# A two-layer decoder trunk on one Trainium2 core: where the sink's exponential lands, and what the turned squares and GpSimd's masks wait for

## The chip, the cores and the metric

The kernel runs on one core of one Trainium2 chip. The core has five engines, each with its own queue of instructions that it works off in order: TensorE (PE in the profile; its loading of weights is listed apart as PEld), VectorE (DVE), ScalarE (ACT), GpSimd (POOL) and SyncE (SP), which here only issues DMA transfers. Data lies in SBUF; matrix products arrive in PSUM, in banks of 512 float32 columns on 128 partitions. The metric is the device time of one execution in microseconds. The kernel before took 1000.27 us, the median of three runs (999.51 to 1000.80).

## What is computed

A trunk of two layers on 512 tokens of width 1024, in float32. Layer A has latent attention with 8 heads, layer B sliding-window attention with 16 query heads on 4 key/value heads, with a learned sink per head; each is followed by an MLP of width 4096 with a squared ReLU. Every sublayer ends in a layer norm of `alpha*x + y`. The part that the change touches is layer B's attention:

```python
def _swa(x, w_q, sinks, w_o, k_band, v_band, rel_bias):
    ...
    s = jnp.where(mask[None, :, None, None], s + bias, -jnp.inf)
    sink = sinks.astype(jnp.float32).reshape(SWA_KV_HEADS, G)[..., None]
    m = jnp.maximum(s.max(-1), sink)
    p = jnp.exp(s - m[..., None])
    denom = p.sum(-1) + jnp.exp(sink - m)
    p = (p / denom[..., None]).astype(x.dtype)
    o = jnp.einsum('bnkgqj,bnjkd->bnqkgd', p, v_band).reshape(B, S, SWA_Q_HEADS * SWA_HEAD_DIM)
    return o @ w_o
```

Queries go in 4 blocks of 128; each block sees the keys of its own block and the one before, 128 back at most.

## The kernel before

**Split factors.** Every float32 operand of a product is held as a high and a low part, and a product is made as two or three matrix products of parts. The helper `split` (L77 and L81) makes the parts: ScalarE copies the source into the high part, and VectorE, or GpSimd where the caller says so, subtracts it from the source to get the low part. All products go through `group` (L105). Weights come in 512 KB pieces by DMA and are split the same way, into tiles `wh` and `wl`; for layer B's query weights from the third piece on and for some pieces of the output projection, GpSimd makes the low part.

**Order.** Instructions are put in order on each engine when the kernel is built, by a planner that simulates the engines with a cost model: of what is ready it takes what comes first in the program, and `high_priority` moves an instruction ahead. `pe(...)` keeps instructions of one engine in program order; all of TensorE's work here is pinned so. `behind((a,))` puts the instructions in its block behind instruction `a` on the same engine. Once built, an engine's order is fixed: an instruction that waits holds all that stand behind it on its engine.

**Layer B's attention.** `run_steps` goes over 16 heads, one step for each. Step u calls `scores(u + 2)`, then pieces of other work from a list (the query projection of two heads at a time, parts of the output projection from step 11 on), then `turn(u)`, and in every second step `mix` for the pair of heads before.

- `scores(h)` makes the four blocks of scores in two PSUM banks `bs[0]` and `bs[1]`, each block with the keys of the block before (128 columns) and its own (128 columns). As exactly one of the two is in reach for each pair of positions, `copy_predicated` (L1426) lays the reachable part of the older block over the own one, so that a head has squares of 128 x 128: one for each query block. VectorE adds the bias and takes the maximum (L1430); `nb` (L1434) is the negated, scaled maximum with the sink. Block 0 has no older block, so the first 128 columns of `bs[0]` are free; the maxima `mx` lie in columns 0 to 3.
- `weigh(h)` takes four exponentials on ScalarE (L1445), each with its sum into `sm`, then the sink's exponential into `ri` (L1449). VectorE adds the two (L1450) and inverts the sum (L1451). GpSimd scales the squares `p` (L1452). For heads 12 to 14, `scores` only appends the head to `waiting`, and `weigh` is called at the end of the next `turn`.
- `turn(h)` transposes the four squares on TensorE (L1468) into a bank of `tbank`, splits it into the tile `pt` (`split`: ScalarE, then VectorE), and GpSimd multiplies three of the squares by the triangle `tri` into `pm` (L1472). For heads 0 to 9 ScalarE's copy in this split is put behind the latest exponential in the program, that of head h + 2 (`state["exp"]`).
- `mix(h)` multiplies the values by `pt` and `pm` of two heads; its first half goes to a bank of `tbank`, its second to one of `bank`. ScalarE copies the upper partitions (L1502, `low`), VectorE adds (L1504, `o`), and `split` with GpSimd makes `oh` and `ol`, the factors of the output projection.

`tbank` has two buffers and `bank` six. [...]

Of the kernel before, what the change touches and what calls it, by code (L numbers as in the profile page):

```python
# [10 lines left out]
AF = mybir.ActivationFunctionType  # L11
# [4 lines left out]
P = 128  # L16
D = 1024
S = 512
NT = S // P
# [6 lines left out]
SQH, SKVH, SHD = 16, 4, 64  # L26
# [22 lines left out]
def build(tc, nc, io, out):  # L49
    with ExitStack() as top:  # L50
# [11 lines left out]
        def nm(s):  # L62
            n_names[0] += 1
            return f"{s}_{n_names[0]}"

        def bank(cols=512, tag="mm", bufs=6):
            return ps.tile([P, cols], F32, tag=tag, bufs=bufs, name=nm(tag), padded_shape=[P, 512])

        def tbank():
            return bank(512, "tr", 2)  # L70

        def f32(ap):
            return ap.bitcast(F32)

        def split(dst_h, dst_l, src, engine=None, keep=False):

            high = nc.scalar.activation(dst_h, src, AF.Copy)  # L77
            if keep:
                pe(high)
            with behind(state.pop("open", None)):  # L80
                low = (engine or nc.vector).tensor_sub(dst_l, src, f32(dst_h))  # L81
            if pinned[0] and engine is None:
                pe(low)
            return high, low

        def pe(ins):
            tc.keep_in_program_order(ins)
# [3 lines left out]
        def behind(pair):  # L91

            both = ExitStack()
            for ins in pair or ():
                both.enter_context(tc.issue_after(ins.ins))
            return both
# [6 lines left out]
        def group(dst, pairs, first=True, last=True, **kw):  # L103
            for i, (st, mv) in enumerate(pairs):
                pe(nc.tensor.matmul(  # L105
                    dst, st, mv, start=first and i == 0, stop=last and i == len(pairs) - 1, **kw
                ))
# [214 lines left out]
        state = {"next": 0, "at": 0, "hold": 0}  # L322
# [32 lines left out]
        class Feat:  # L355
# [11 lines left out]
            def turn(self, t):  # L367
                turn_tokens(t, self)
# [59 lines left out]
        sink = cp.tile([P, SQH], F32, name="sink")  # L428
# [167 lines left out]
        def run_steps(units, ahead, scores, turn, mix, fill, per, lag, rest):  # L596

            total = sum(f[0] for f in fill)  # L600
            n, spent, at = len(units), 0.0, 0
            for u in range(-ahead, n):
                if u + ahead < n:
                    scores(*units[u + ahead])
                target = total * (u + ahead + 1) / (n + ahead)
                while at < len(fill) and (spent < target or fill[at][1] <= u) and fill[at][2] <= u:
                    fill[at][3]()
                    spent += fill[at][0]
                    at += 1
                if u < 0:  # L610
                    continue
                turn(*units[u])
                if u >= lag and (u - lag) % per == per - 1:
                    mix(units[u - lag][0])
            for f in fill[at:]:
                f[3]()
            for f in rest:
                f()
            for u in range(n, n + lag):
                if (u - lag) % per == per - 1:  # L620
                    mix(units[u - lag][0])
# [338 lines left out]
        with tc.tile_pool(name="mla", bufs=1) as mp:  # L960
# [123 lines left out]
            for t in range(NT):  # L1084
# [12 lines left out]
                if t == 2:  # L1097
                    with tc.high_priority():
                        pt = tbank()
# [186 lines left out]
            for t in range(2):  # L1286
                for kp in range(3):
                    fill.append((1.3, 99, max(8 * kp + 10, 29 * t), lambda t=t, kp=kp: proj.part(t, kp)))
                    if t == kp == 0:
# [3 lines left out]
            state["hold"] = hold  # L1293
            head_queries(1)
            run_steps([(h, i) for h in range(H) for i in range(NT)], AHEAD_S, scores, turn, mix, fill, NT, 2,
                      [lambda kp=kp: proj.part(2, kp) for kp in range(2)])

# [18 lines left out]
        with tc.tile_pool(name="swa", bufs=1) as mp:  # L1316
# [56 lines left out]
            bias = [None] * 8  # L1373
# [24 lines left out]
                    nc.scalar.activation(q[own, cols], b[own, :], AF.Copy)  # L1398
                    nc.vector.tensor_sub(q[other, cols], b[own, :], f32(q[own, cols]))  # L1399

            ps_of = [None] * SQH
            pts = [None] * 8

            def scores(h, _):
                j = h // GRP
                q = qs[h]
                nb = sp.tile([P, NT], F32, tag="nb", bufs=3, name=nm("nb"))
                sm = sp.tile([P, NT], F32, tag="sm", bufs=3, name=nm("sm"))
                ri = sp.tile([P, NT], F32, tag="ri", bufs=3, name=nm("ri"))
                bs = []  # L1410
                for n2 in range(2):
                    b = bank().rearrange("p (a b) -> p a b", a=2)
                    bs.append(b)
                    for a in range(2):
                        n = 2 * n2 + a
                        lo_c = P if n == 0 else 0
                        kc = slice(0, P) if n == 0 else slice((n - 1) * P, (n + 1) * P)
                        tq = slice(n * P, (n + 1) * P)
                        group(b[:, a, lo_c:], [(q[:, tq], khh[j][:, kc]), (q[:, tq], kll[j][:, kc])])

                mx = bs[0][:, 0, 0:NT]
                for n2 in range(2):
                    at = slice(1 - n2, 2)
                    b = bs[n2][:, at, :]
                    other = upper.bitcast(mybir.dt.int16)[:, None, :].broadcast_to([P, n2 + 1, P])
                    nc.vector.copy_predicated(b[:, :, P:], other, b[:, :, 0:P])  # L1426
                    for a in range(2):
                        n = 2 * n2 + a
                        own = bs[n2][:, a, P:]
                        nc.vector.tensor_tensor_reduce(  # L1430
                            out=own, in0=own, in1=bias[h // 2][:, h % 2, P:] if n == 0 else bias[h // 2][:, h % 2, 0:P],
                            op0=ALU.add, op1=ALU.max, scale=1.0, scalar=NEG, accum_out=mx[:, n : n + 1],
                        )
                nc.vector.tensor_scalar(nb, mx, sink8[:, h : h + 1], -SWA_SCALE, ALU.max, ALU.mult)  # L1434
                if 12 <= h < 15:
                    waiting.append((h, bs, nb, sm, ri))
                else:
                    weigh(h, bs, nb, sm, ri)

            waiting = []  # L1440

            def weigh(h, bs, nb, sm, ri):
                p = mp.tile([P, NT, P], F32, tag="p", bufs=3, name=nm("p"))
                for n in range(NT):
                    state["exp"] = nc.scalar.activation(  # L1445
                        p[:, n, :], bs[n // 2][:, n % 2, P:], AF.Exp, bias=nb[:, n : n + 1],
                        scale=SWA_SCALE, accum_out=sm[:, n : n + 1],
                    )
                nc.scalar.activation(ri, nb, AF.Exp, bias=sink[:, h : h + 1])  # L1449
                nc.vector.tensor_add(sm, sm, ri)  # L1450
                nc.vector.reciprocal(ri, sm)  # L1451
                nc.gpsimd.tensor_mul(p, p, ri.unsqueeze(2).broadcast_to([P, NT, P]))  # L1452
                ps_of[h] = p

            def turn(h, _):
                m, a = h // 2, h % 2
                p = ps_of[h]
                if a == 0:
                    whole = mp.tile([P, 2, NT, 2, P], F32R, tag="pt", bufs=2, name=nm("pt"))
                    if m % 2:  # L1460
                        part = mp.tile([P, 2, NT - 1, 2, P], F32R, tag="pm", bufs=1, name=nm("pm"))
                    else:
                        part = gp.tile([P, 2, NT, 2, P], F32R, tag="gb", bufs=1, name=nm("pm"))[:, :, 1:]
                    pts[m] = whole, part
                whole, part = [z[:, :, :, a, :] for z in pts[m]]
                pt = tbank().rearrange("p (a b) -> p a b", a=NT)
                for n in range(NT):
                    pe(nc.tensor.transpose(pt[:, n, :], p[:, n, :], ident))  # L1468
                with behind((state["exp"],) if h < 10 else None):
                    split(whole[:, 0], whole[:, 1], pt)  # L1470
                own = tri[:, None, None, :].broadcast_to([P, 2, NT - 1, P])
                nc.gpsimd.tensor_mul(part, f32(whole[:, :, 1:]), own)  # L1472
                if waiting:
                    weigh(*waiting.pop())

            def mix(h):
                m, j = h // 2, h // GRP
# [172 lines left out]
```

## Time and profile before

| | us |
|---|---|
| median of three runs (999.51 to 1000.80) | 1000.27 |
| the profiled execution | 999.92 |
| its span, from first to last instruction | 998.1 |

| engine | busy in the span, us | in instructions |
|---|---|---|
| TensorE, products (PE) | 981.4 | 6028 |
| VectorE (DVE) | 780.5 | 1279 |
| ScalarE (ACT) | 545.0 | 842 |
| GpSimd (POOL) | 240.6 | 207 |

Layer B's attention with its first head's scores to its last mix lies between 536 and 636 us of the span. The granted clock of TensorE is 0.999 of full speed over the span.

How to read the rows that follow. A row of a timeline has the start and the duration in us, the engine, the line and the operation, the tile written and the tiles read, their shapes, how many instructions are merged in it, and in brackets the idle time of the engine just before it with what ended that. The name `tr` stands for banks of `tbank`, `mm` for banks of `bank`, also where these hold `mix`'s products. A row of waits says who waited for whom, the sum in us, how often, and the longest. A row of stretches has for each engine the busy time in us and the count of instructions, then the granted clock, the share of DMA and GB/s. A row of groups has the count, the busy time with the mean in ns, and the idle time before. A row of a tile has the shortest, median and longest duration in ns. The chain of waits is what ended last, followed back; "issue" in it is time for which the profile shows no cause.

### The profile page before, as it was taken

The numbers are of one execution on the slowest core, as the hardware profiler recorded it, in microseconds if no ns is written. First come the engines' busy times: TensorE is split into PE (matmuls) and PEld (weight loads), VectorE is DVE, ScalarE is ACT, GpSimd is POOL, SyncE is SP. The second block draws the span as 40 slices with busy tenths as digits, with TensorE's granted clock in tenths as the row PEclk, the third lists the DMA queues.
The fourth block names the chain that finished last, engine by engine and source line by source line (L and its number), as shares of the span: only waits on it lengthen the run. The fifth ranks groups of instructions, "written<-read, shape, count | busy, mean of one in ns | idle before, by whom it ended". The sixth has DMA issues, their size and how long they took to land.

```text
span 998.1 us, 15676 instructions
## 1 busy us (share of the span) xinstructions
PE 981.4 (98%) x6028; PEld 881.4 (88%) x6028; DVE 780.5 (78%) x1279; ACT 545.0 (55%) x842; POOL 240.6 (24%) x207
## 2 busy tenths in 40 slices
PE   9999999999999999999999987999999999999997
PEld 9888888998898999998898876889998999999986
DVE  6589858989679779785686888698885986898756
ACT  5557643567447537646146776436763664664620
POOL 0231101121312212210003887622131122122000
PEclk9999999999999999999999999999999999999999
DMA  7421236399789878954132224237996897898332
GB/s 261 141 91 43 89 123 202 53 214 245 137 206 224 157 169 236 222 91 148 64 106 96 85 70 153 81 89 129 272 190 117 231 217 118 221 263 146 83 127 84
DMA packets 60678, 149.54 MB, mean 150 GB/s; under 512 B 5259, under 2 KB 10300, under 8 KB 60604
## 3 DMA queue, kind: packets, MB, share of 16 engines
q0 software_dynamic: 24320, 58.73, 33.5%
q1 hardware_dynamic: 36140, 89.56, 26.2%
q8 instruction: 47, 0.77, 0.3%
q14 instruction: 27, 0.22, 0.1%
q10 hardware_dynamic: 144, 0.26, 0.1%
HBM read 146.41 MB, written 4.22 MB: 151 GB/s over the span
## 4 chain that ended last, share of the span: by engine, by line
PE 90%; DVE 5%; ACT 3%; issue 1%; POOL 1%; DMA 0%; DVEq 0%; ACTq 0%; POOLq 0%
PE mm L105 83%; PE tr L105 5%; ACT p L1445 1%; DVE sm L1450 1%; DVE o L1504 1%; PE tr L1243 1%; DVE mm L1430 1%; PE tr L742 1%; DVE pt L81 0%; POOL wl L81 0%; DVE mm L1426 0%; ACT wh L77 0%; DMA raw<-in_w_h 0%; PE tr L507 0%; DVE q L1399 0%
## 5 line engine op out<-in xcount | busy, mean ns | idle before, releaser
L105 PE MATMUL mm<-wh,fac 128*128 128x512 f32 (+1 forms) x944 | 292.6, 386 | 0.0
L77 ACT ACTIVATE wh<-wq 128x1024 fp32r<-128x1024 f32 x164 | 173.7, 1060 | 184.6 <-PE mm L105 133.3
L81 DVE TENSOR_TENSOR wl<-wq,wh 128x1024 fp32r<-128x1024 f32 x164 | 199.5, 1220 | 69.6 <-ACT wh L77 68.8
L105 PE MATMUL mm<-xth,wh 128*128 128x256 f32 (+1 forms) x928 | 243.5, 290 | 0.2 <-DVE o L1504 0.2
L105 PE MATMUL mm<-xth,wl 128*128 128x256 f32 (+1 forms) x800 | 233.3, 292 | 0.0
L105 PEld LDWEIGHTS mm<-wh,fac 128*128 128x128 f32 x944 | 176.3, 188 | 35.5 <-DVE fac L81 0.6
L105 PE MATMUL mm<-xtl,wh 128*128 128x256 f32 (+1 forms) x672 | 197.1, 293 | 0.0
L105 PE MATMUL mm<-wl,fac 128*128 128x512 f32 (+1 forms) x472 | 182.3, 386 | 0.0
L105 PEld LDWEIGHTS mm<-xth,wh 128*128 128x128 f32 x928 | 168.6, 192 | 3.4 <-ACT wh L77 0.3
L105 PEld LDWEIGHTS mm<-xth,wl 128*128 128x128 f32 x800 | 153.2, 192 | 2.7
L105 PEld LDWEIGHTS mm<-xtl,wh 128*128 128x128 f32 x672 | 128.7, 191 | 3.0
L77 ACT ACTIVATE wh<-raw 128x1024 fp32r<-128x1024 f32 (+3 forms) x86 | 84.9, 988 | 80.4 <-PE mm L105 54.3
L204 POOL DMA_DIRECT2D wq<-in_up x64 | 77.6, 1238 | 199.5 <-DVE wl L81 192.3
L105 PEld LDWEIGHTS mm<-wl,fac 128*128 128x128 f32 x472 | 88.8, 188 | 16.6
L81 DVE TENSOR_TENSOR wl<-raw,wh 128x1024 fp32r<-128x1024 f32 (+2 forms) x64 | 74.7, 1176 | 31.0 <-ACT wh L77 30.2
L204 POOL DMA_DIRECT2D wq<-in_down x48 | 42.0, 875 | 189.8 <-DVE wl L81 184.0
L81 POOL TENSOR_TENSOR wl<-raw,wh 128x1024 fp32r<-128x1024 f32 (+2 forms) x22 | 47.0, 2138 | 88.0 <-ACT wh L77 65.2
L105 PE MATMUL mm<-wh,oh 128*128 128x512 f32 x128 | 50.8, 397 | 0.0
L105 PE MATMUL mm<-wh,ol 128*128 128x512 f32 x128 | 50.2, 392 | 0.6 <-POOL ol L81 0.6
L443 POOL TENSOR_TENSOR rs<-mv,half 128x1 f32<-128x1 f32 x16 | 10.0, 623 | 166.9 <-DVE mv L488 162.2
L105 PE MATMUL mm<-wl,oh 128*128 128x512 f32 x128 | 50.0, 391 | 0.1
L641 DVE TENSOR_TENSOR x<-mm,x 128x512 f32<-128x512 f32 (+1 forms) x49 | 32.9, 675 | 15.2 <-PE mm L105 15.1
(246 smaller groups left out, 1796.1 us busy)
## 6 DMA issues: line engine op xcount, KB each, us to landing
wq<-in_up POOLq DMA_DIRECT2D x64, 512.0 KB, 7.4
wq<-in_down POOLq DMA_DIRECT2D x48, 512.0 KB, 7.3
wq<-in_up SPq DMA_DIRECT2D x32, 512.0 KB, 6.5
raw<-in_down SPq DMA_DIRECT2D x28, 512.0 KB, 5.7
wq<-in_down SPq DMA_DIRECT2D x24, 512.0 KB, 5.3
raw<-in_up SPq DMA_DIRECT2D x16, 512.0 KB, 4.9
raw<-in_w_o SPq DMA_DIRECT2D x8, 512.0 KB, 3.4
raw<-in_w_sq SPq DMA_DIRECT2D x8, 512.0 KB, 3.2
```

What stands on the lines that cost most here:

```text
L77: high = nc.scalar.activation(dst_h, src, AF.Copy)
L81: low = (engine or nc.vector).tensor_sub(dst_l, src, f32(dst_h))
L105: pe(nc.tensor.matmul(dst, st, mv, start=first and i == 0, stop=last and i == len(pairs) - 1, **kw))
L204: state["added", key, a, more, jp] = nc.gpsimd.dma_start(half(a, jp), chunk(*more, jp), accum_op=ALU.add)
L443: state["rs"] = nc.gpsimd.tensor_tensor(r, v, half, ALU.pow)
L641: nc.vector.tensor_add(xs[t][:, c], b, xs[t][:, c])
L742: pe(nc.tensor.transpose(pt[:, a, :], xs[t][:, k * P : (k + 1) * P], ident))
L1243: pe(nc.tensor.transpose(pt[:, kb * P : (kb + 1) * P], p[:, kb * P : (kb + 1) * P], ident))
L1430: nc.vector.tensor_tensor_reduce(out=own, in0=own, in1=bias[h // 2][:, h % 2, P:] if n == 0 else bias[h // 2][:, h % 2, 0:P], op0=ALU.add, ...
L1445: state["exp"] = nc.scalar.activation(p[:, n, :], bs[n // 2][:, n % 2, P:], AF.Exp, bias=nb[:, n : n + 1], scale=SWA_SCALE, accum_out=sm[: ...
L1450: nc.vector.tensor_add(sm, sm, ri)
L1504: nc.vector.tensor_add(o[to, n2, :].rearrange("p (n q) -> p n q", n=2), parts[lo, :, a, :], low[:, :, a, :],)
```

## The change

Three things are changed, all in layer B's attention. `turn` no longer puts its split behind exponentials, and the deferral of `weigh` for heads 12 to 14 is gone: `scores` always calls `weigh`. The sink's exponential is written to columns 4 to 7 of `bs[0]`, and VectorE's sum reads it there; `ri` then only holds the inverse. GpSimd's scaling is given high priority and kept in `muls`, and the mask of head h is put behind the scaling of head h + 1 on GpSimd's queue. The instructions that are executed are the same in kind and number.

```diff
-            ps_of = [None] * SQH
+            ps_of, muls = [None] * SQH, [None] * SQH
...
                 nc.vector.tensor_scalar(nb, mx, sink8[:, h : h + 1], -SWA_SCALE, ALU.max, ALU.mult)
-                if 12 <= h < 15:
-                    waiting.append((h, bs, nb, sm, ri))
-                else:
-                    weigh(h, bs, nb, sm, ri)
-
-            waiting = []
+                weigh(h, bs, nb, sm, ri)
 
             def weigh(h, bs, nb, sm, ri):
                 p = mp.tile([P, NT, P], F32, tag="p", bufs=3, name=nm("p"))
                 for n in range(NT):
-                    state["exp"] = nc.scalar.activation(
+                    nc.scalar.activation(
                         p[:, n, :], bs[n // 2][:, n % 2, P:], AF.Exp, bias=nb[:, n : n + 1],
                         scale=SWA_SCALE, accum_out=sm[:, n : n + 1],
                     )
-                nc.scalar.activation(ri, nb, AF.Exp, bias=sink[:, h : h + 1])
-                nc.vector.tensor_add(sm, sm, ri)
+                own = bs[0][:, 0, NT : 2 * NT]
+                nc.scalar.activation(own, nb, AF.Exp, bias=sink[:, h : h + 1])
+                nc.vector.tensor_add(sm, own, sm)
                 nc.vector.reciprocal(ri, sm)
-                nc.gpsimd.tensor_mul(p, p, ri.unsqueeze(2).broadcast_to([P, NT, P]))
+                with tc.high_priority():
+                    muls[h] = nc.gpsimd.tensor_mul(p, p, ri.unsqueeze(2).broadcast_to([P, NT, P]))
                 ps_of[h] = p
...
                     pe(nc.tensor.transpose(pt[:, n, :], p[:, n, :], ident))
-                with behind((state["exp"],) if h < 10 else None):
-                    split(whole[:, 0], whole[:, 1], pt)
+                split(whole[:, 0], whole[:, 1], pt)
                 own = tri[:, None, None, :].broadcast_to([P, 2, NT - 1, P])
-                nc.gpsimd.tensor_mul(part, f32(whole[:, :, 1:]), own)
-                if waiting:
-                    weigh(*waiting.pop())
+                with behind((muls[h + 1],) if h + 1 < SQH else None):
+                    nc.gpsimd.tensor_mul(part, f32(whole[:, :, 1:]), own)
```

## The prediction

> **What bounds the kernel now.** I read the engines and the 40 slices of the page first, to find where TensorE (PE) is not busy; then busy time by stretches, the waits of PE, the timeline of one pair of heads, and the chain of waits.
>
> ```profile
> PE 981.4 (98%) x6028; PEld 881.4 (88%) x6028; DVE 780.5 (78%) x1279; ACT 545.0 (55%) x842; POOL 240.6 (24%) x207
> PE   9999999999999999999999987999999999999997
> ```
>
> PE is the bound of the whole, idle for 998.1 - 981.4 = 16.7 us. Apart from the last slice, it drops below 9 tenths only in two slices near 575 to 625 us: layer B's attention, where every edit lies.
>
> ```profile
> core 0: us, PE busy (x) PEld busy (x) DVE busy (x) ACT busy (x) POOL busy (x), PEclk, DMA share, GB/s
> 550.00:570.00 20.00, 19.20 (x118) 16.72 (x117) 16.26 (x59) 12.91 (x41) 18.47 (x11) 1.00 0.32 107
> 570.00:605.00 35.00, 31.25 (x188) 26.89 (x187) 30.78 (x106) 24.92 (x80) 28.33 (x19) 1.00 0.33 112
> 605.00:630.00 25.00, 19.20 (x110) 15.65 (x110) 19.74 (x60) 15.58 (x52) 16.35 (x12) 1.00 0.18 66
> 581.37:592.77 11.40, 10.14 (x62) 8.75 (x61) 9.76 (x35) 8.20 (x26) 9.32 (x7) 1.00 0.20 70
> ```
>
> PE's idle time is 0.80, 3.75 and 5.80 us in the three stretches: 10.35 us, the most that the change can win while PE's work stays. The last row is one pair of heads, from the transposes of head 6 to those of head 8: 10.14 us of PE's work take 11.40, and no engine is full. What PE waited for in these 80 us (us in total, times, longest):
>
> ```profile
> PE tr L105 <- DVE pt L81: 7.4, 5, 2.2
> PE mm L105 <- DVE q L1399: 1.1, 1, 1.1
> PE tr L105 <- DVE nb L1434: 0.8, 1, 0.8
> PE mm L105 <- POOL ol L81: 0.6, 1, 0.6
> PE tr L1468 <- POOL p L1452: 0.3, 1, 0.3
> ```
>
> Four fifths is `mix` (the tile `tr` at L105) waiting for the split of turned squares (`pt`): `mix` takes its first bank from `tbank`, which has two, so it needs the bank of the head turned two uses earlier, free once VectorE (DVE) has made the low part. The pair from the timeline:
>
> ```profile
> 581.37 0.60 PE L1468 MATMUL tr<-ident,p 128*128 128x128 f32 x4
> 584.08 0.35 ACT L1445 ACTIVATE p<-mm,nb 128x128 f32<-128x128 f32 x1
> 585.63 0.59 ACT L77 ACTIVATE pt<-tr 128x512 fp32r<-128x512 f32 x1
> 586.25 0.59 ACT L1398 ACTIVATE q<-mm 64x512 fp32r<-64x512 f32 x1
> 586.54 0.66 DVE L81 TENSOR_TENSOR pt<-tr,pt 128x512 fp32r<-128x512 f32 x1
> 586.77 1.04 POOL L1452 TENSOR_TENSOR p<-p,ri 128x512 f32<-128x512 f32 x1 [0.45 <-DVE ri L1451]
> 587.24 0.69 DVE L1399 TENSOR_TENSOR q<-mm,q 64x512 fp32r<-64x512 f32 x1
> 587.35 0.70 PE L105 MATMUL tr<-pt,vv 128*128 128x512 f32 x2 [1.26 <-DVE pt L81]
> 587.77 1.86 POOL L1472 TENSOR_TENSOR pm<-pt,tri 128x768 fp32r<-128x768 f32 x1
> 588.60 1.04 DVE L1450 TENSOR_TENSOR sm<-sm,ri 128x4 f32<-128x4 f32 x1 [0.67 <-ACT ri L1449]
> 590.10 1.04 POOL L1452 TENSOR_TENSOR p<-p,ri 128x512 f32<-128x512 f32 x1 [0.47 <-DVE ri L1451]
> ```
>
> Head 6 is turned at 581.97, but ScalarE (ACT) splits it at 585.63, behind head 8's exponentials: the written wait. And the sum of four numbers at L1450 takes 1.04 us: it ends at 589.64, when GpSimd's (POOL) mask ends (587.77 + 1.86 = 589.63). The tile's view, with `nb`, an operation as small that reads the bank, and a group row:
>
> ```profile
> L1450 DVE TENSOR_TENSOR sm<-sm,ri x13: 164/1016/1828, 557.8 to 623.0; 128x4 f32<-128x4 f32 x13
> L1434 DVE TENSOR_SCALAR nb<-mm,sink x13: 208/221/224, 555.7 to 621.0; 128x4 f32<-128x4 f32 x13
> L1450 DVE TENSOR_TENSOR sm<-sm,ri 128x4 f32<-128x4 f32 x13 | 12.2, 942 | 4.8 <-ACT ri L1449 4.6
> ```
>
> The sum takes 0.16 us at best and 1.83 at worst. The chain of waits runs through ACT and DVE here, not PE:
>
> ```profile
> 584.08 1.48 ACT p L1445 x8
> 585.56 0.19 ACT ri L1449
> 588.60 1.05 DVE sm L1450
> 595.50 1.48 ACT p L1445 x8
> ```
>
> From one exponential of a pair to the next pair's is 11.42 us, with a stopped sum in it.
>
> **The change part by part.** **The sink's exponential into the bank.** No instruction is added or removed; L1449 writes and L1450 reads four columns of PSUM in place of SBUF. The sum then has one input in SBUF, like `q<-mm,q`: the row at 587.24 takes 0.69 us though the mask starts in its midst. I price the sum at `nb`'s 0.22; ends 0.16 and today's 0.94. For 13 sums that frees 12.2 - 13 x 0.22 = 9.3 us of DVE, of which a pair's chain holds 1.04 - 0.22 = 0.82. ACT's write into a bank has no row; between the sink's exponential as it stands in the chain (0.19) and one of 128 columns (0.35), I take 0.19, as nothing about its length changes; 0.16 more for 13 heads would be 2.1 us of ACT's work, inside its idle time. The 0.06 us by which a bank read exceeds 0.16 (13 x 0.06 = 0.8) lie in DVE's idle time, 11.40 - 9.76 = 1.64 a pair; without that cover 0.8 would be lost.
>
> ```profile
> 589.07 0.22 PE L105 MATMUL mm<-skh,q 128*128 128x128 f32 x1
> 607.01 0.58 ACT L77 ACTIVATE pt<-tr 128x512 fp32r<-128x512 f32 x1
> 609.64 1.86 POOL L1472 TENSOR_TENSOR pm<-pt,tri 128x768 fp32r<-128x768 f32 x1 [2.81 <-DVE pt L81]
> 609.68 1.83 DVE L1450 TENSOR_TENSOR sm<-sm,ri 128x4 f32<-128x4 f32 x1
> 609.71 0.70 PE L105 MATMUL tr<-pt,vv 128*128 128x512 f32 x2 [2.16 <-DVE pt L81]
> 612.44 0.69 DVE L1399 TENSOR_TENSOR q<-mm,q 64x512 fp32r<-64x512 f32 x1
> 613.19 0.39 PE L105 MATMUL mm<-skh,q 128*128 128x256 f32 x1 [1.14 <-DVE q L1399]
> 619.24 0.69 PE L105 MATMUL tr<-pt,vv 128*128 128x512 f32 x2 [1.60 <-DVE pt L81]
> 622.99 1.28 DVE L1450 TENSOR_TENSOR sm<-sm,ri 128x4 f32<-128x4 f32 x1 [1.16 <-ACT ri L1449]
> 628.95 0.50 PE L105 MATMUL mm<-wh,ol 128*128 128x512 f32 x1 [0.63 <-POOL ol L81]
> ```
>
> The bank is held longer: from the last exponential that reads it to the sum. Head 8's exponentials start at 584.08, so its sum can end by 584.08 + 1.48 + 0.19 + 0.22 = 585.97; head 10's scores start at 589.07, so some 3 us remain. [...]
>
> **No wait for the exponentials (heads 0 to 9).** ACT's split, 0.62 us from start to start (585.63 to 586.25), leaves its place between two heads' exponentials. ACT idles 11.40 - 8.20 = 3.20 us a pair; if the split fits there, the chain is 11.42 - 0.82 - 0.62 = 9.98 us, below PE's 10.14, and a pair gains 11.40 - 10.14 = 1.26. If it stays on the chain elsewhere, 11.42 - 0.82 = 10.60 remain and a pair gains 0.80. I take 1.1, nearer the first, because of the 3.20. Three pairs lie in 570 to 605: **3.3 us** (2.4 to 3.75). In 550 to 570 the one wait of 0.80 is of the same kind, with weight splits in ACT's way: **0.6** (0 to 0.8).
>
> **Heads 12 to 14 weigh at once.** The exponentials lose their place behind the turn of two heads earlier, so they come before its split in the program. The 2.16 us (head 10's split, at 607.01) and the 1.60 (head 12's) were not held by the removed wait. They may lose to exponentials of 1.48 + 0.19 = 1.7 us, or win what an earlier split gives. I take **0.5** of 3.76, with ends -1.7 and +2.6. The 1.14 us is due to the stopped sum at 609.68, ahead of the query's split: 1.61 us freed there cover it, **1.1** (0 to 1.14). The 0.63 us before the output projection stand behind the sum at 622.99, with 1.06 freed: **0.6** (0 to 0.63). Of the small waits, **0.2** (0 to 0.44).
>
> **Masks behind the next scaling.** No operation is added. Scaling 8 (586.77) stood before mask 6 (587.77); now only scaling 7 must. So mask 6 can move up as far as its split does, 3.7 us (585.63 - 581.97), with POOL's weight splits, output splits and scaling 8 then queued behind it. POOL is busy 9.32 us a pair, in a pair of 10.14: 92%. It costs nothing while POOL's 11.40 - 9.32 = 2.08 idle us hide its waits. No DMA is issued from this loop on POOL; SP's loads follow released tiles and come earlier with the rest.
>
> **Sum:** 3.3 + 0.6 + 0.5 + 1.1 + 0.6 + 0.2 = 6.3 us; by the ends 0.7 to 9.4. The profiled execution took 999.92 us, span 998.1 and 1.8 around it, 0.35 under the median 1000.27. So the span becomes 991.8 and the median 1000.3 - 6.3 = **994.0**, its own range 990.9 to 999.6.
>
> **The rivals.**
> - **GpSimd becomes the bound (slower).** Its order is fixed beforehand. A mask placed early waits at the head for DVE's low part, with the next scaling behind it, hence the next transposes. The price is shown at 609.64: 2.81 us idle for `pt`. 9.32 + w exceeds 11.40 from w = 2.08; at 2.81 a pair takes 12.13, 0.73 more, over seven pairs 5.1: **1005.4**. For it: 92%; against: low parts should come earlier, and scaled squares are early (head 8's at 587.81, used at 592.77), so 5 us of lateness are covered.
> - **ACT's order gives back most.** A split waiting for PE's transposes stands before exponentials, and late heads' exponentials stand before splits: 1.7 us lost twice leave 6.3 - 0.5 - 3.4 = 2.4 or so: **997.9**. For it: two of the five long waits were never held by the wait; against: head 8's exponentials start 2.1 us after head 6 is turned (584.08 - 581.97), room for a split of 0.62.
> - **The sum stays stopped.** Then 11.42 - 0.62 = 10.80 a pair, 0.6 x 3 = 1.8 won, less 1.7 in the late heads: about **1000.2**. Against: `q<-mm,q`. [...]
>
> **How the numbers follow.** Forecast 0.68, POOL 0.12, ACT's order 0.12, sum stopped 0.08. About 0.2% (2 us) can be told from no change. Faster: 0.65 of the forecast, 0.06 of ACT's order, 0.02 of the last, 0.73. Slower: POOL's 0.12 and 0.02 of the last, 0.14; within: 0.13. The range 990.5 to 1000.5 takes in all but POOL's case and small parts beyond the ends.
>
> **What would show it.** Right: `sm<-mm,sm` near 0.22 us for all heads; ACT's `pt` of heads 2 to 9 within 1 us of its transposes; PE's wait for `pt` from 7.4 to under 3 us; pairs near 10.3; PE's work the same. Wrong: `sm` above 0.5 us, scaling waiting behind a mask, PE waiting for `p`, or PE's idle time moving to after 605 us or into the output projection.

## The result, and the profile after

The changed kernel takes 992.78 us (median of four runs, 990.84 to 993.60) beside 1000.07 for the kernel before in the same set (999.51 to 1000.80). The ratio is 0.9924, with a 95% interval of 0.9907 to 0.9941: 7.3 us less. The forecast was 994.0, 6.3 us less. The profiled execution took 993.60 us, with a span of 991.8 us; the forecast of the span was the same number, but made up of other parts, as will be seen: that it was met to the tenth is luck.

Busy time by stretches of the kernel after comes first. The rows are cut at its own events: 600.67 is where the transposes of head 11 start, and 582.58 to 592.48 is one pair, from one `mix` to the next.

```profile
core 0: us, PE busy (x) PEld busy (x) DVE busy (x) ACT busy (x) POOL busy (x), PEclk, DMA share, GB/s
550.00:570.00 20.00, 20.00 (x123) 17.62 (x122) 16.32 (x68) 14.16 (x44) 19.24 (x12) 1.00 0.24 81
570.00:600.67 30.67, 30.67 (x186) 26.88 (x185) 26.32 (x103) 24.12 (x79) 28.16 (x19) 1.00 0.37 125
600.00:605.00 5.00, 1.97 (x12) 1.50 (x10) 3.17 (x8) 3.18 (x11) 2.88 (x2) 0.93 0.73 294
605.00:610.00 5.00, 4.97 (x20) 4.68 (x21) 3.77 (x17) 3.10 (x12) 1.33 (x2) 0.50 0.29 105
610.00:630.00 20.00, 19.08 (x108) 16.34 (x107) 9.73 (x38) 10.79 (x33) 15.54 (x11) 0.97 0.00 1
582.58:592.48 9.90, 9.90 (x63) 8.72 (x61) 8.70 (x37) 8.10 (x27) 9.30 (x7) 1.00 0.23 80
```

Up to head 11 TensorE has no gap at all; a pair takes 9.90 us where it took 11.4. Then, between 600 and 605, it is busy for 1.97 of 5 us, and in the 5 us behind that its granted clock is 0.50. All its waits from 545 to 640 us are two:

```profile
PE mm L105 <- ACT p L1440: 3.1, 1, 3.1
PE tr L105 <- DVE pt L81: 0.9, 1, 0.9
```

The five long waits for `pt` (7.4 us) have become one of 0.9; a wait of a kind that wasn't there before, for exponentials, takes 3.1. Here is head 6 again, from the timeline of the kernel after:

```profile
578.10 0.60 PE L1465 MATMUL tr<-ident,p 128*128 128x128 f32 x4
...
579.64 0.58 ACT L77 ACTIVATE pt<-tr 128x512 fp32r<-128x512 f32 x1
580.64 0.35 ACT L1440 ACTIVATE p<-mm,nb 128x128 f32<-128x128 f32 x1
...
581.05 0.69 DVE L81 TENSOR_TENSOR pt<-tr,pt 128x512 fp32r<-128x512 f32 x1
...
582.58 0.71 PE L105 MATMUL tr<-pt,vv 128*128 128x512 f32 x2
582.81 1.86 POOL L1469 TENSOR_TENSOR pm<-pt,tri 128x768 fp32r<-128x768 f32 x1
...
583.66 0.16 DVE L1446 TENSOR_TENSOR sm<-mm,sm 128x4 f32<-128x4 f32 x1
```

ScalarE splits 0.94 us after the transposes end (579.64 - 578.70) where it was 3.66, ahead of the exponentials of head 8; `mix` starts without a wait; and the sum takes 0.16 us in the middle of a mask of GpSimd that lasts until 584.67; in the kernel before, the sum at 588.60 took 1.04 us and ended with such a mask (589.64 and 589.63). The tile's row for the 13 heads in this stretch:

```profile
L1446 DVE TENSOR_TENSOR sm<-mm,sm x13: 152/161/163, 557.4 to 617.4; 128x4 f32<-128x4 f32 x13
```

And the new wait, from the timeline: SyncE's loads, ScalarE and TensorE.

```profile
592.75 0.97 SPq L217 DMA_DIRECT2D wq<-in_up  x2
593.82 0.88 SPq L142 DMA_DIRECT2D raw<-in_w_so  x2
...
601.77 1.06 ACT L77 ACTIVATE wh<-raw 128x1024 fp32r<-128x1024 f32 x1 [2.05 <-DMA raw<-in_w_so]
602.86 0.59 ACT L1398 ACTIVATE q<-mm 64x512 fp32r<-64x512 f32 x1
603.47 0.37 ACT L1440 ACTIVATE p<-mm,nb 128x128 f32<-128x128 f32 x1
...
605.03 1.22 PE L105 MATMUL mm<-pt,vv 128*128 128x256 f32 x4 [3.06 <-ACT p L1440]
```

ScalarE's queue has the split of an output weight piece (`w_so`) ahead of head 12's exponentials. The piece is loaded behind two pieces of the up projection, 512 KB each, and arrives at 601.77; ScalarE stands still for 2.05 us, the exponentials come late, and `mix` of heads 8 and 9 waits for the bank that they free. In the kernel before the same split started at 605.43 behind other work, with no wait for its load.

What this did to the total is seen in two stretches: from the transposes of head 4 to those of head 10, and from there to those of head 15. First the kernel before, then the kernel after:

```profile
569.78:604.19 34.41, 30.66 (x181) 26.30 (x180) 30.21 (x103) 24.95 (x79) 28.39 (x19) 1.00 0.31 104
604.19:629.29 25.10, 19.30 (x111) 15.79 (x110) 20.52 (x64) 15.70 (x51) 15.80 (x13) 1.00 0.21 79
568.19:597.91 29.72, 29.72 (x181) 26.18 (x180) 25.33 (x103) 24.29 (x78) 28.44 (x20) 1.00 0.29 96
597.91:623.15 25.24, 21.26 (x111) 18.32 (x110) 16.08 (x63) 15.67 (x51) 15.60 (x12) 0.86 0.28 108
```

The steady pairs win 4.69 us. The late heads win nothing: TensorE's idle time falls from 5.80 to 3.98 us, but the same products (111 in both traces) take 21.26 us in place of 19.30, at a granted clock of 0.86. The span is 6.3 us shorter: the rest lies between the transposes of head 0 and head 4 (0.96 us), ahead of head 0 (0.63) and behind head 15 (0.16). For the 0.63 no run shows a cause.

### The profile page after: what moved, and what is told of

It reads as the page before. It is cut to its first block, busy times and chain, and to the rows that moved or that the text cites. A ratio compares the mean times of both kernels' runs of the same rounds, so it can differ in the third digit from the quotient of the medians.

```text
span 991.8 us, 15665 instructions
## 1 busy us (share of the span) xinstructions
PE 981.9 (99%) x6028; PEld 883.7 (89%) x6028; DVE 770.5 (78%) x1279; ACT 544.7 (55%) x842; POOL 238.9 (24%) x207
## 4 chain that ended last, share of the span: by engine, by line
PE 97%; DMA 1%; DVE 1%; POOL 0%; ACT 0%; issue 0%; SPq 0%; DVEq 0%; POOLq 0%
PE mm L105 89%; PE tr L105 5%; PE tr L1243 1%; DMA raw<-in_w_so 1%; PE tr L742 1%; PE tr L1465 1%; PE tr L507 0%; POOL wl L81 0%; PE tr L1007 0%; PE mm L1148 0%; ACT p L1440 0%; DVE pt L81 0%; DVE mm L1430 0%; DVE x L481 0%; ACT wh L77 0%
```

## The experiments

Twelve kernels were run, each beside the kernel before. The rivals at this point: A, only the place of the split counts; B, only the sum counts; against my theory that both carry the gain.

**Each edit alone.** The bank alone, applied to the kernel before:

```diff
-                nc.scalar.activation(ri, nb, AF.Exp, bias=sink[:, h : h + 1])
-                nc.vector.tensor_add(sm, sm, ri)
+                own = bs[0][:, 0, NT : 2 * NT]
+                nc.scalar.activation(own, nb, AF.Exp, bias=sink[:, h : h + 1])
+                nc.vector.tensor_add(sm, own, sm)
```

> The kernel before with the first edit alone: the sink's exponential goes to the bank; the wait of heads 0 to 9, the deferral of heads 12 to 14 and GpSimd's order stay. Theory (both edits carry the gain): the sums fall to 0.16 us, a pair in the steady stretch takes about 10.6 us in place of 11.4, PE still waits 0.4 to 0.9 us a pair for the turned squares, and the time is 994.5 to 996.5. Rival A (only the place of the split counts, the stopped sum lies beside the path): sums at 0.16 but the time 999 to 1000.5. Rival B (only the sum counts): 992 to 993.5, pairs at 10.1.

Measured: 1000.01 us, ratio 0.9993 (0.9984 to 1.0002). That is rival A's number, and not my theory's. But the trace does not agree with rival A. From stretches, the waits and ScalarE's timeline of this kernel:

```profile
583.85:594.23 10.38, 10.14 (x60) 8.75 (x61) 8.39 (x35) 8.11 (x27) 9.30 (x7) 1.00 0.22 79
605.00:610.00 5.00, 2.99 (x12) 2.83 (x13) 4.78 (x18) 4.10 (x17) 4.06 (x4) 0.68 0.34 117
615.00:620.00 5.00, 1.54 (x6) 1.45 (x7) 2.18 (x14) 3.65 (x19) 5.00 (x5) 0.70 0.00 0
```

```profile
PE tr L1469 <- POOL p L1453: 4.1, 1, 4.1
PE tr L105 <- DVE pt L81: 4.0, 1, 4.0
```

```profile
602.56 1.06 ACT L77 ACTIVATE wh<-raw 128x1024 fp32r<-128x1024 f32 x1 [4.03 <-DMA raw<-in_w_so]
```

A pair takes 10.38 us in place of 11.40, so the sum is on the path and 1 us a pair is won. All of it is lost after 600 us: ScalarE waits 4.03 us for the same output weights, TensorE waits twice for 4 us, and its clock is down to about 0.7 around these waits. This made the late load the first suspect.

The two waits alone (the `behind` of heads 0 to 9 and the deferral of heads 12 to 14 out of the kernel before, as in the change):

> The kernel before with the wait of heads 0 to 9 and the deferral of heads 12 to 14 taken away, nothing else: the sum stays in SBUF. Theory: sums stay at about 1 us in the median, a pair takes about 10.8 us, and the late heads give part back: 997.5 to 1000. Rival A (only the split): 992 to 994. Rival B (only the sum): 999.5 to 1001.

Measured: 996.17 us, ratio 0.9954 (0.9941 to 0.9966), better than my theory and short of rival A. The pair of this kernel, and its sums:

```profile
575.78:586.59 10.81, 10.16 (x64) 8.79 (x62) 9.36 (x34) 7.89 (x27) 9.12 (x7) 1.00 0.21 75
```

```profile
L1445 DVE TENSOR_TENSOR sm<-sm,ri x16: 150/330/2358, 540.8 to 621.9; 128x4 f32<-128x4 f32 x16
```

The pair is as expected (10.8). The sums are stopped less often than expected (median 0.33 us, but up to 2.36); one of the two sums of a pair still takes 1.00 us. The same with the third edit, which is the changed kernel with the sum back in SBUF:

```diff
-                own = bs[0][:, 0, NT : 2 * NT]
-                nc.scalar.activation(own, nb, AF.Exp, bias=sink[:, h : h + 1])
-                nc.vector.tensor_add(sm, own, sm)
+                nc.scalar.activation(ri, nb, AF.Exp, bias=sink[:, h : h + 1])
+                nc.vector.tensor_add(sm, sm, ri)
```

> The changed kernel with the sum in SBUF again, the other two edits as they are. Theory: sums stopped by GpSimd's instructions again (median about 1 us), steady pairs at 10.5 to 11, 996.5 to 999.5. Rival A (only the split): 992 to 994, whatever the sums take.

Measured: 995.91 us, ratio 0.9957 (0.9945 to 0.9970): slower than the whole change, so rival A falls. It is 0.6 us below the expected range, and the median of the sums was 0.31 us where 1 was expected.

**The third edit.** The changed kernel without it:

```diff
-                with tc.high_priority():
-                    muls[h] = nc.gpsimd.tensor_mul(p, p, ri.unsqueeze(2).broadcast_to([P, NT, P]))
+                nc.gpsimd.tensor_mul(p, p, ri.unsqueeze(2).broadcast_to([P, NT, P]))
...
-                with behind((muls[h + 1],) if h + 1 < SQH else None):
-                    nc.gpsimd.tensor_mul(part, f32(whole[:, :, 1:]), own)
+                nc.gpsimd.tensor_mul(part, f32(whole[:, :, 1:]), own)
```

> The changed kernel without the third edit: GpSimd's scaling has no high priority and the masks are not put behind it. Theory (the third edit only fixes an order that comes about anyway): 992 to 993.8. Rival C (masks, now early, would get ahead of the scalings on GpSimd, which is busy 92% of a pair): over 995, with PE waiting for p.

Measured: 991.86 us, ratio 0.9916 (0.9903 to 0.9930). The interval overlaps with that of the whole change: the third edit has no effect on the whole change that these runs can tell. What it does beside other orders of the late heads was not tried.

**The wait put back**, in the changed kernel:

```diff
-                    nc.scalar.activation(
+                    state["exp"] = nc.scalar.activation(
...
-                split(whole[:, 0], whole[:, 1], pt)
+                with behind((state["exp"],) if h < 10 else None):
+                    split(whole[:, 0], whole[:, 1], pt)
```

> The changed kernel with the wait of heads 0 to 9 back, the deferral still gone, the sum in the bank, the masks behind the scalings. Theory (both edits carry the gain): pairs at 10.4 to 10.7 us with PE waiting 0.3 to 0.6 us for the turned squares, 993.5 to 996. Rival B (only the sum counts): the same as the changed kernel within 1 us, 992 to 993.5.

Measured: 997.21 us, ratio 0.9973 (0.9964 to 0.9982); rival B falls. The pair's row and the two longest waits:

```profile
583.18:593.58 10.40, 10.15 (x60) 8.77 (x61) 8.39 (x35) 8.13 (x27) 9.30 (x7) 1.00 0.22 76
```

```profile
PE tr L105 <- DVE pt L81: 3.5, 1, 3.5
PE tr L1465 <- POOL p L1449: 2.5, 1, 2.5
```

The pair is as expected; the time lies above the expected range, with late waits as with the bank alone (ScalarE stands 3.6 us for the output weights).

**What the new wait is due to.** The deferral put back in the changed kernel:

```diff
-                weigh(h, bs, nb, sm, ri)
+                if 12 <= h < 15:
+                    waiting.append((h, bs, nb, sm, ri))
+                else:
+                    weigh(h, bs, nb, sm, ri)
+
+            waiting = []
...
+                if waiting:
+                    weigh(*waiting.pop())
```

> The changed kernel with the deferral of heads 12 to 14 back and nothing else. Theory (the 3.1 us that PE waits after head 11's transposes come from a late load of output weights, with ScalarE's queue behind it, not from the order of weighing): the wait moves by less than 1 us and the time stays 991 to 994. Rival D (the wait is due to the exponentials of head 12 having lost their place): the wait falls under 1 us, the clock stays at 1.00, and the time is 986 to 989.5.

Measured: 991.68 us, ratio 0.9915 (0.9901 to 0.9928). The wait for the exponentials is 2.1 us and one of 0.8 for scaled squares has come; rival D falls, and the order of weighing is not its cause. The order of the loads, in the changed kernel:

```diff
-            fill.append((0, 11, 11, preloads[1]))
...
+                if (t, kp) == (0, 1):
+                    fill.append((0, 12, 12, preloads[1]))
```

> The changed kernel with the first two loads of layer B's up projection (512 KB each) issued after the next two loads of output weights on SyncE's queue, not ahead of them. Theory (the output weights arrive late, as two loads stand ahead of them): the wait of 3.1 us for the exponentials falls under 1 us, the granted clock no longer drops in the 5 us behind it, and the time is 986 to 989.5. Rival D (the deferral's order makes the wait): the wait stays at 2 us or more and the time at 991 to 994.

Measured: 990.68 us, ratio 0.9905 (0.9892 to 0.9919). From the timeline, then the waits of this kernel:

```profile
591.99 0.88 SPq L142 DMA_DIRECT2D raw<-in_w_so  x2
592.92 0.94 SPq L217 DMA_DIRECT2D wq<-in_up  x2
...
597.07 1.06 ACT L77 ACTIVATE wh<-raw 128x1024 fp32r<-128x1024 f32 x1 [0.34 <-PE mm L105]
```

```profile
PE tr L1465 <- POOL p L1449: 2.2, 1, 2.2
PE tr L105 <- DVE pt L81: 1.3, 1, 1.3
PE mm L105 <- DVE o L1499: 0.4, 1, 0.4
```

The wait for the load and that for the exponentials are gone, and the clock of the profiled execution is 1.00 throughout: so the late load made them. But the time is above the expected range of 986 to 989.5, since other waits of 3.9 us in all come in the same place. That is as much as the 4.0 us of the changed kernel. What the profiled execution wins in the late heads is the clock:

```profile
597.11:619.66 22.55, 18.62 (x111) 15.93 (x110) 16.11 (x63) 15.58 (x51) 15.71 (x12) 1.00 0.32 121
```

This stretch takes 2.69 us less than in the changed kernel (25.24), of which TensorE's work is 2.64 (21.26 - 18.62). In time the two kernels can't be told apart by these runs: the intervals overlap, and the runs whose mean clock is 1.000 take 990.84 us in the changed kernel and 989.75 and 990.03 in this one.

If the late load is also what hid the bank's share, the bank alone must win with the new order of loads, and the kernel before must not:

> The kernel before with the sink's exponential in the bank, and the two loads of the up projection behind the next two loads of output weights on SyncE's queue. Theory (the bank alone does speed up the pairs, to 10.4 us, and loses it to the late output weights, the waits behind them and the clock's drop): no wait of ScalarE for these weights, clock 1.00, 993.5 to 996.5. Rival E (the bank alone wins nothing at the end, whatever the loads): 998.5 to 1001.

> The kernel before with only the order of the loads changed. Theory (it reaches these weights 3 to 4 us later than the faster kernels and doesn't wait for them): 999 to 1001. Rival F (the order of the loads is a gain of its own in any kernel): 996 to 998.5.

> The changed kernel with the sum in SBUF again and the order of the loads changed. ScalarE waited 1.6 us for the weights in this kernel without the new order. Theory: 993.5 to 996, pairs at 10.8; so the bank's share beside the split, measured without the late load, is 3.5 to 5.5 us. Rival A (only the place of the split counts): 990 to 992, like the changed kernel with the new order of loads.

The three are the kernels named above with the edit to the loads (`sbuf_later` is the changed kernel with the sum in SBUF). All of it in one table (us, and the ratio to the kernel before with its interval):

| | loads as they were | output weights first |
|---|---|---|
| kernel before | 1000.1 to 1000.7 | 999.13, 0.9987 (0.9979 to 0.9996) |
| bank alone | 1000.01, 0.9993 (0.9984 to 1.0002) | 996.06, 0.9956 (0.9942 to 0.9970) |
| change, sum in SBUF | 995.91, 0.9957 (0.9945 to 0.9970) | 995.37, 0.9948 (0.9935 to 0.9960) |
| whole change | 992.78, 0.9924 (0.9907 to 0.9941) | 990.68, 0.9905 (0.9892 to 0.9919) |

The bank alone gains 4.0 us from the new order of loads (1000.01 - 996.06), so rival E falls. The kernel before gains about 1.2, less than rival F asked for. Its trace does not give the loads as the reason: its profiled execution is 1.36 us ahead of the kernel before at the transposes of head 0 (549.22 and 550.58), before the loads that changed places are issued (596.00), and takes as long from there to those of head 15 (78.65 and 78.71).

The late load is not all that hides the bank's share, however. With the bank alone and the new order, the wait for the turned squares falls from 4.0 to 1.5 us, but the one for scaled squares stays, and against expectation so does a slow clock behind it (a row of waits and one of stretches):

```profile
PE tr L1469 <- POOL p L1453: 4.0, 1, 4.0
615.00:620.00 5.00, 5.00 (x20) 4.52 (x19) 2.18 (x6) 1.79 (x3) 3.48 (x3) 0.50 0.00 0
```

The squares are those of head 13. Their inverse is ready at 611.29, but on GpSimd's queue a low part of `o` and a mask stand ahead of the scaling, which starts at 613.60. No run takes this apart.

In the right column the bank is worth 3.1 us alone (999.13 - 996.06), the split 3.8 (999.13 - 995.37) and both 8.5 (8.2 by the ratios, as the last kernel was measured in another set). The last is more than the sum of the two: by 1.2 us in the ratios, which is no more than their intervals allow, and by 3.5 in the profiled executions from head 0 to head 15 (1.7, 3.0 and 8.2). It is not because of the steady pairs. From the transposes of head 4 to those of head 10 the four kernels take 34.39, 31.17, 31.60 and 29.72 us: the bank wins 3.2, the split 2.8 and both 4.7, less than the sum, as TensorE's own work is reached. The surplus comes from the stretches beside them, where each edit alone runs into waits and a slow clock: the bank alone in the late heads, as just shown (27.27 us for the 25.06 of the kernel before), and the kernel with the sum in SBUF in the first four heads (21.94 us for 19.20), where one sum takes 2.37 us (from 560.62) and ends with a low part of weights on GpSimd (from 560.59, 2.38 us). TensorE's wait of 1.98 us behind it and the clock of 0.66 that follows are shown in the last section.

**The waits that remain.** The new order of loads and the deferral together:

> The changed kernel with the new order of loads and the deferral of heads 12 to 14 back. With the new order alone TensorE still waited 2.2 us for scaled squares and 1.3 us for turned ones after head 10. Theory (the two waits stem from the order of the late heads' work on VectorE and ScalarE, where splits stand behind exponentials): the deferral puts splits first and the sum of waits goes from 3.9 to 2 to 3 us, 988.5 to 990.5. Rival (each order of the late heads costs as much): 990 to 992.

Measured: 992.51 us, ratio 0.9918 (0.9904 to 0.9931), with the same waits of 2.2, 1.3 and 0.4 us as without the deferral, and a clock of 0.66 in one stretch of 5 us (610 to 615). My theory of these waits fell. The chain of waits of the kernel with the new order of loads has this piece, the low part of the fourth output weight piece:

```profile
598.54 1.13 DVE wl L81
```

Given to GpSimd, in the kernel with the new order of loads:

```diff
-POOL_O, POOL_SO = (0, 2), (0, 1, 2, 6, 7)
+POOL_O, POOL_SO = (0, 2), (0, 1, 2, 3, 6, 7)
```

> The changed kernel with the new order of loads, and the low part of the fourth output weight piece made by GpSimd in place of VectorE. With the new order of loads the time was 990.7, less gain than expected: TensorE waited 2.2 us for scaled squares and 1.3 us for turned ones at heads 10 to 13. Theory (the late heads are bound by a chain through VectorE, on which this piece takes 1.13 us): the two waits together fall from 3.5 to 2.5 us or less, and the time is 988.5 to 990.3. Rival G (GpSimd is busy enough that its 2.4 us for the piece delay the scalings): the wait for scaled squares grows, 990.7 to 993.

Measured: 988.99 us, ratio 0.9892 (0.9875 to 0.9908), the fastest of all: 3.8 us below the changed kernel. The waits:

```profile
PE tr L1465 <- POOL p L1449: 0.9, 1, 0.9
PE tr L105 <- DVE pt L81: 0.4, 1, 0.4
PE mm L105 <- POOL ol L81: 0.4, 1, 0.4
```

The two waits fell from 3.5 to 1.3 us, and the stretch from head 10 to head 15 from 22.55 to 20.93, as expected if the late heads are bound through VectorE; rival G falls. GpSimd had just enough room for the 2.4 us: it is now busy all the time from 600 to 610. The intervals of the two times still overlap.

## Why the prediction was right

- **The bound of the steady pairs: right, and the gain larger than its limit.** Freed sum and moved split together took the chain below TensorE's work, as the working said (9.98 against 10.14). The transposes of head 4 to those of head 10 took 604.19 - 569.78 = 34.41 us before and 597.91 - 568.19 = 29.72 after: 4.69 us, where I had put 3.3 and at most 3.75. In 550 to 570 it was also more than the whole wait, about 1.0 for 0.6. The mis-sized term is TensorE's work: all 3.75 us of idle time went, and with them 0.94 us of busy time (30.66 to 29.72 for the same 181 products), which is 0.24 of the 10.14 in the pair that was looked at. So the 10.35 us of idle time were not the most that could be won. The sign for the split was not met by all heads: ScalarE starts it 0.1 to 2.2 us after the transposes of heads 2 to 9 and not always within 1 us, and the pairs close up all the same. Of the idle time, 7.4 of 10.35 us were waits for `pt`: seven tenths, not the four fifths that the working says.
- **The price of each edit in a pair: right for the split, small for the sum.** 11.42 - 0.62 = 10.80 was worked out for the split alone; 10.81 was measured. For the sum alone 10.60 was worked out; 10.38 was measured.
- **The sum's length:** 0.16 us and not `nb`'s 0.22. The lower end held.
- **The late heads: wrong.** I put 0.5 + 1.1 + 0.6 + 0.2 = 2.4 us there. From the transposes of head 10 to those of head 15 it took 25.10 us before (604.19 to 629.29) and 25.24 after (597.91 to 623.15): nothing was won. The waits of 1.14 and 0.63 us did go, as did the 2.16 and the 1.60, but a wait of 3.06 for a late load and 0.92 for `pt` came in their place, 1.8 us less in all, and at the lower clock behind the first TensorE's work took 1.96 us longer. The step that failed is the sentence on the loads, that SyncE's "come earlier with the rest": the output weights were issued 4.6 us earlier (593.82 for 598.41), as were the two pieces ahead of them, and ScalarE was ready for them 5.7 us earlier (599.72 for 605.43); they took until 601.77. In the trace of the kernel before, these weights land 3.4 to 9.3 us after they are issued (585 to 615), which was not set against ScalarE's new schedule. The sum also had no term for the clock. With the output weights loaded first, the late heads took 22.55 us, 2.55 less than before, close to the 2.4; the waits that remain there are others than the working had. The total came out right as a surplus of 1.39 us from head 4 to head 10, 0.4 ahead of these and 0.8 outside the heads nearly cancel a shortfall of 2.5.
- **GpSimd as the bound: fell.** It is busy 9.30 of 9.90 us in a pair and TensorE never waits for `p` in the changed kernel. In other orders of the late heads it does, 2.2 us with the output weights loaded first.
- **ScalarE's order gives back:** in part. It happened in the late heads, but through a load, and not through exponentials ahead of splits; putting the deferral back won nothing beyond the intervals.
- **The sum stays stopped:** fell with the 13 sums of 0.152 to 0.163 us, as the 0.69 us of `q<-mm,q` beside a mask had suggested.
- **The bank held longer:** no wait on it was seen in the changed kernel; the one bank that TensorE waited for was late for the weights' sake, as the new order of loads showed.

## What to carry to other kernels

When a chain through several engines is shortened, look at each load whose reader comes earlier: a transfer with slack in the old schedule can take the gain back, by the wait and by a slow clock behind it (here 3.06 us, then 0.50 of full speed for about 6), and an edit that wins 3 us where it acts (10.38 us a pair for 11.40, in three pairs) then measures as nothing (1000.01 us). So test an edit alone, but read its trace in the stretch that it touches before calling it worthless, and compare TensorE's work as well as its idle time. VectorE's sum of four numbers took 1.04 us here with both inputs in SBUF beside a mask of GpSimd (0.16 to 1.83 over 13 heads); with one of its inputs in a PSUM bank it took 0.15 to 0.16.

## What the runs showed of the hardware

TensorE's granted clock fell to 0.50 behind the wait of 3.06 us: rows of products of 512 columns start 0.43 us apart instead of 0.23, for about 6 us (605.03 to 611.17). The four runs of the changed kernel have mean clocks of 0.996, 0.995, 0.997 and 1.000, and the last is the fastest, 990.84 us beside 992.25 to 993.60: some 1.4 to 2.8 us are at stake, though no run here isolates them. Waits of much the same length don't always bring it: in the changed kernel with the sum in SBUF and the new order of loads, a wait of 1.98 us did, as the row of TensorE's wait and the stretch behind it show,

```profile
564.29 0.70 PE L105 MATMUL tr<-pt,vv 128*128 128x512 f32 x2 [1.98 <-DVE nb L1434]
```

```profile
565.00:570.00 5.00, 5.00 (x25) 4.57 (x25) 3.03 (x13) 2.60 (x10) 4.01 (x3) 0.66 0.38 148
```

while 2.16 us in the kernel before and 2.21 in the changed kernel with the new order of loads left it at 1.00. What decides between them no run here shows.

ScalarE's sink exponential took 0.25 to 0.29 us into the bank where it had taken 0.30 into SBUF, and VectorE's sum was hardly slower for reading the bank (median 0.16 us) than the fastest sum in SBUF (0.15 us).
